# Merged FFN products grouped by their column count, and three small moves at the start of a two-layer decoder trunk

## The chip, the core and the metric

The kernel runs on one core of one Trainium2 chip. The metric is the device time of one execution in microseconds (us). The times given are medians over executions; the profile is of one execution. Engines are named as the profile names them: PE (TensorE) with its weight loads PEld, DVE (VectorE), ACT (ScalarE), POOL (GpSimd) and SP (SyncE). A suffix q, as in SPq, stands for the engine's own queue of issued work, here its DMA issues.

## The reference

The kernel computes two decoder layers on 256 positions of width 1024. Each layer is a half-step SwiGLU FFN, an attention, and a second half-step FFN, each behind an RMS norm whose shift, scale and gate are computed from a vector c:

```python
def swiglu(h, w_gate, w_up, w_down):
    return (jax.nn.silu(h @ w_gate) * (h @ w_up)) @ w_down

c_act = jax.nn.silu(c)
for layer in range(2):
    sh1, sc1, g1, sh2, sc2, g2, sh3, sc3, g3 = jnp.split(c_act @ ada_w[layer] + ada_b[layer], 9, axis=-1)
    h = modulate(rms_norm(x, norm_g[layer, 0]), sh1, sc1)
    x = x + 0.5 * g1 * swiglu(h, ffn_w_gate[layer, 0], ffn_w_up[layer, 0], ffn_w_down[layer, 0])
    h = modulate(rms_norm(x, norm_g[layer, 1]), sh2, sc2)
    x = x + g2 * (moba_attention(h, ...) if layer == 0 else mla_attention(h, ...))
    h = modulate(rms_norm(x, norm_g[layer, 2]), sh3, sc3)
    x = x + 0.5 * g3 * swiglu(h, ffn_w_gate[layer, 1], ffn_w_up[layer, 1], ffn_w_down[layer, 1])
```

The FFN's inner width is 2816. All inputs and weights are float32.

## The kernel before

**Products in parts.** Every float32 matrix that enters a large product is split into a high part hi, rounded to a type that PE takes at full rate, and a rest lo: ACT writes hi (L629), DVE writes lo = raw - hi (L630), both for 128x1024 pieces in `split`. A product is then hi·hi + hi·lo + lo·hi. `mm3` (L759 to L761) issues these as three products.

**Merged blocks.** In the gate and up projections of all four FFNs, once past the first columns, the weights are the stationary operand and the activations h stand beside each other as [h_hi | h_lo], 2 x 256 columns. `mm2` issues one product of 512 columns with the weights' hi part (L863), which gives hi·hi and hi·lo in the two halves of a PSUM tile, and one of 256 columns with the weights' lo part (L864) into the second half. For each of 128 inner columns f there are two sides, gate and up, of KD = 8 contraction steps k each; two values of f share a weight block. Four sides of eight k make a block. `units` then adds the halves (L904, L905), applies Silu (L907), multiplies (L908) and splits again (`split_evac`, L774 and L775).

**Down projection.** The rest of an FFN multiplies the split inner activations by w_down in products of 512 columns, with `mm3`.

**First stage.** `first` computes the first six blocks of 128 inner columns of the first FFN while x and the weights of the shift and scale vectors arrive. It broadcasts Silu(c) over the partitions into c_b with a product (L1531) and two ACT copies (L1532), forms the sums of squares of the two row blocks of x on DVE (L1545), reduces weights against c_b on DVE (L640), and from these makes h (z at L1576) and multiplies it (L1594 to L1596) in products of 256 columns.

**The order of the work.** The program is first written in one order and then ordered anew by a planner, `Order`: it simulates the engines with a table of costs and writes each engine's instructions in the order of that plan. Engines run their queues in that order. Instructions in `held` are not placed before 40 us of the plan (`HELD`); `hold` marks them: the tables of the rotary embedding (`rope_tables`) and `mla_consts`, the products of those tables with gains (L1347) and two masks. `ranked` puts first-stage instructions in a given rank. Loads are issued by SP; a buffer pool `splitp` has eight hi and eight lo tiles, and PSUM has four tiles for these products.

Of the kernel before, what the change touches and what calls it, by code (L numbers as in the profile page):

```python
# [15 lines left out]
AF = mybir.ActivationFunctionType  # L16
ALU = mybir.AluOpType
# [5 lines left out]
D = 1024  # L23
KD = D // P
S = 256
# [15 lines left out]
EPS = 1e-6  # L41
# [145 lines left out]
HELD = 40e3  # L187
# [56 lines left out]
class Order:  # L244
# [120 lines left out]
    def place(self, need):  # L365

        n = len(self.ins)
        left, ready, start, done = list(self.npre), [0.0] * n, [0.0] * n, [0.0] * n
# [26 lines left out]
        def consider(k):  # L395

            r = ready[k]
            for t in self.tiles_of[k]:
                if t not in granted:
                    waiting.setdefault(t, []).append(k)  # L400
                    if t not in asked:
                        asked[t] = True
                        grant(self.ring[t])
                    return
                r = max(r, granted[t] + (WAKE if granted[t] else 0.0))
            if self.ins[k].name in self.held:
                r = max(r, HELD)
            ready[k] = r
            heapq.heappush(known[self.eng[k]], (r, k))

        def choose(e, t):
# [24 lines left out]
        while placed < n:  # L436
            t, e = 1e15, None
            for x in ENGINES:
                if x == "SP" and len(flight) >= FLIGHT:
                    free[x] = max(free[x], flight[-FLIGHT] + 50.0)  # L440
                if avail[x] or known[x]:
                    s = free[x] if avail[x] else max(free[x], known[x][0][0])
                    if s < t:
                        t, e = s, x
            assert e, "no instruction can be placed"
            while known[e] and known[e][0][0] <= t:
                r, k = heapq.heappop(known[e])
# [6 lines left out]
            k = x[1]  # L454
# [18 lines left out]
            for s in self.succ[k]:  # L473
                if self.eng[s] != e or self.dma[k]:
                    r = done[k] + WAKE
                else:
                    r = t + occ if e == "PE" else done[k] + 35.0
# [8 lines left out]
            for u in self.tiles_of[k]:  # L486
                users[u] -= 1
                last_use[u] = max(last_use.get(u, 0.0), done[k])
                r = self.ring[u]
# [34 lines left out]
def trunk(ctx: ExitStack, tc: tile.TileContext, a: dict, out: bass.AP):  # L524
    nc = tc.nc
# [41 lines left out]
    def pe(us):  # L567
        clock[0] += us
        if busy[0]:
            return  # L570
        while pend and pend[0][0] <= clock[0]:
            run_next()
        while pace[0] and clock[0] >= pace[1]:
            pace[1] += pace[0]
            ada(1)
# [4 lines left out]

    first_rank, held, late, last_ffn = {}, set(), set(), []

    @contextmanager
    def noted(names):
        n = len(nc.cur_bb.bb.instructions)
        yield
        names.update(i.name for i in nc.cur_bb.bb.instructions[n:])
# [20 lines left out]
    xs = [cp.tile([P, D], F32, name=f"x{t}") for t in range(NT)]  # L610
# [3 lines left out]
    all_cols = cp.tile([P, 3 * NK + KD + NT + 4 + 2 * RO], F32, name="cols")  # L614
# [5 lines left out]
    cols, cact = all_cols[:, :3 * NK].rearrange("p (i c) -> p i c", i=3), places["c"]  # L620
    m_cols = cp.tile([P, 2, NK], F32, name="m_cols")

    c_b = cp.tile([P, D], F32, name="c_b")
# [24 lines left out]
    ready = set()  # L648
# [208 lines left out]
        both = h[0][3][:, k].rearrange("p i t q -> p (i t q)")  # L857
        return both[:, :S], both[:, S:], both

    def mm2(ps, wh, wl, h, start, stop):  # L860


        nc.tensor.matmul(ps, wh, h[2], start=start, stop=False)  # L863
        nc.tensor.matmul(ps[:, S:], wl, h[0], start=False, stop=stop)  # L864
        pe(0.347)

    def norm_T(t, key, *more):
        h = new_h(t)
        modulate_T(t, [(key, h), *more], rstd_of(t), CHAIN)
# [16 lines left out]
    def ffn(layer, idx, h, after, ada_to, start=None):  # L886

        last = (layer, idx) == (1, 1)
        with ExitStack() as st:
# [4 lines left out]
            def units(f, gate, up=None):  # L894


                g = gp.tile([P, S], F32, tag="gT", name=nm("g"), bufs=2)
                if up is None:
                    gate, up = gate[:, :S], gate[:, S:]
                    nc.scalar.activation(g, gate, AF.Silu)  # L900
                else:
                    u = gp.tile([P, S], F32, tag="uT", name=nm("u"), bufs=1 if start else 2)
                    for x, ps in ((g, gate), (u, up)):
                        nc.scalar.activation(x, ps[:, S:], AF.Copy)  # L904
                        nc.vector.tensor_tensor(x, ps[:, :S], x, op=ALU.add)  # L905
                    up = u
                    nc.scalar.activation(g, g, AF.Silu)  # L907
                nc.vector.tensor_tensor(g, up, g, op=ALU.mult)  # L908
                gh, gl = [gq.tile([P, S], F32R, tag=f"{nme}{f}", name=nm(nme)) for nme in ("gh", "gl")]
                split_evac(gh, gl, g)  # L910
                for t in range(NT):
                    gT[f, t] = kslice(gh, t), kslice(gl, t)
# [6 lines left out]
            for t in range(0 if start else NT):  # L919
                for i, pl in enumerate(parts):  # L920
                    ps = mm_tile()
# [22 lines left out]
            for f0 in range(B1 * P if start else FB, F, S):  # L944
                if f0 == SIDE_TO * S:
                    while start and next(side[0], "end") != "end":
                        bias_step()
                    gq = st.enter_context(tc.tile_pool(name=nm("gp"), bufs=1))
                if start and f0 == ROPE_AT * S:
                    hold(rope_tables)  # L950
                    hold(mla_consts)
                parts = [[], []]
                for f in range(f0 // P, (f0 + S) // P):
                    merged = (layer, idx) in MERGED
                    ps = [mm_tile() for _ in range(1 + merged)]
                    for i, pl in enumerate(parts):
                        for k in range(KD):
                            if len(pl) <= k:
                                pl += nextw()
                            w = [w[:, f * P - f0:(f + 1) * P - f0] for w in pl[k]]  # L960
                            hs = hk_both(h, k)
                            if merged:
                                mm2(ps[i], *w, hs, start=k == 0, stop=k == KD - 1)
                            else:
                                mm3(ps[0][:, i * S:(i + 1) * S], *w, *hs[:2], start=k == 0, stop=k == KD - 1)
                            if start and k in HOOKS and f0 < SIDE_TO * S:
                                bias_step()
                    units(f, *ps)
            for half in range(2):
                acc = [mm_tile() for _ in range(NT)]  # L970
                wl = []
# [223 lines left out]
                yield  # L1195
            drain()

    def hold(fn):

        with noted(held):  # L1200
            fn()

    def bias_step():

        if len(groups) < 2:
            hold(lambda: next(side[0], None))
        if groups:
            later(BIAS_WAIT, groups.pop(0))
# [280 lines left out]
    def first(units):  # L1489
# [5 lines left out]
        with ExitStack() as st:  # L1495
# [15 lines left out]
                    nc.sync.dma_start(w1(k, j), a["first"][k, j])  # L1511

            with ranked(0):
                nc.sync.dma_start(c_b[0:1, :], a["c"])
                nc.sync.dma_start(all_cols, a["cols"])
            for t in range(NT):
                with ranked(t):
                    nc.sync.dma_start(xs[t], a["x"][0, t * P:(t + 1) * P, :])
# [22 lines left out]
            for t in range(NT):  # L1541
                with ranked(1):
                    s = stats[t] = small([P, 1], "ssq0")
                    junk = raws[3 + t]
                    nc.vector.tensor_tensor_reduce(junk, xs[t], xs[t], 1.0 / D, EPS, op0=ALU.mult, op1=ALU.add,  # L1545
                                                   accum_out=s)
                    diag.append(fp.tile([P, P], F32, name=nm("diag")))
                    rs.append(rstd_of(t))
                    nc.scalar.activation(diag[t], ident, AF.Copy, scale=rs[t])
# [20 lines left out]
            for k in range(KD):  # L1570
# [19 lines left out]
                for f in range(B1):  # L1590
                    for i in range(2):
                        c = (2 * f + i) * P
# [55 lines left out]
```

## Time and profile before

| | |
|---|---|
| runs (us) | 1000.14, 1002.26, 1004.02 |
| median (us) | 1002.26 |
| profiled execution (us) | 1002.69 |
| its span in the profile (us) | 1000.9 |
| PE, PEld busy (us) | 986.4, 836.7 |
| DVE, ACT, POOL busy (us) | 850.1, 629.1, 82.5 |
| DMA over the span | 260.53 MB, mean 260 GB/s |

How to read it: a group's row names the line, engine and operation, output and inputs, shapes and count; after the bar come the busy time of the group, the mean of one in ns, and the idle time of the engine before them with what ended it. A timeline row has start and length in us. A row of one line's summary has the count, the shortest, median and longest duration in ns, and the first and last start. A row by windows has the window, its length, the busy time with the count, the granted TensorE clock, the share of the DMA engines and GB/s. Matmuls are pipelined, so their durations overlap.

### The profile page before, as it was taken

How to read it: one execution, taken by the hardware profiler on the slowest of the kernel's cores; microseconds unless marked ns; L12 is line 12 of the kernel's file. 1: busy time of each engine (PE TensorE's matmuls, PEld its weight loads, DVE VectorE, ACT ScalarE, POOL GpSimd, SP SyncE). 2: the span in 40 equal slices, each digit the busy share in tenths (PEclk: the TensorE clock that was granted, in tenths of full speed). 3: DMA queues.
4: the chain of work that ended last, by engine and by line, in shares of the span. 5: the costliest groups of instructions: out<-in, count | busy, mean ns of one | idle time of the engine just before them, and what ended most of it. 6: DMA issues, size and time to landing. Idle time of an engine off the chain costs nothing.

```text
span 1000.9 us, 15247 instructions
## 1 busy us (share of the span) xinstructions
PE 986.4 (99%) x5558; PEld 836.7 (84%) x5558; DVE 850.1 (85%) x1443; ACT 629.1 (63%) x1169; POOL 82.5 (8%) x124
## 2 busy tenths in 40 slices
PE   8999999999999999999999999999999999999998
PEld 6988888878888788888888888888888878888886
DVE  7999999799989899999799999944998789667642
ACT  5688665378755875665367666643879696566521
POOL 3011000022231000000000000000143010000000
PEclk9999999999999999999999999999999999999999
DMA  9978999899786688988988998552343467544630
GB/s 349 405 281 311 332 311 334 303 335 355 267 309 226 239 281 338 335 317 293 367 320 303 343 326 323 210 213 103 105 153 126 170 242 269 204 168 168 229 129 22
DMA packets 54237, 260.53 MB, mean 260 GB/s; under 512 B 6289, under 2 KB 6801, under 8 KB 35986
## 3 DMA queue, kind: packets, MB, share of 16 engines
q1 hardware_dynamic: 52850, 256.06, 70.5%
q0 software_dynamic: 1024, 3.17, 1.1%
q8 instruction: 43, 0.70, 0.3%
q10 hardware_dynamic: 288, 0.33, 0.1%
q14 instruction: 32, 0.26, 0.1%
HBM read 255.34 MB, written 4.19 MB: 259 GB/s over the span
## 4 chain that ended last, share of the span: by engine, by line
PE 78%; issue 9%; DVE 7%; DMA 4%; ACT 1%; POOL 0%; SPq 0%; DVEq 0%; ACTq 0%; POOLq 0%
PE mm L863 23%; PE mm L759 12%; PE mm L761 12%; PE mm L760 12%; PE mm L864 11%; DVE lo L630 2%; PE at L1014 2%; DMA adaw<-in_ada_dram 2%; DMA raw<-in_first_dram 1%; PE at L1070 1%; PE at L1050 1%; PE tr L809 1%; DMA raw<-in_w_dram 1%; PE tr L1169 1%; DVE z L825 0%
## 5 line engine op out<-in xcount | busy, mean ns | idle before, releaser
L630 DVE TENSOR_TENSOR lo<-raw,hi 128x1024 fp32r<-128x1024 f32 (+3 forms) x312 | 369.6, 1203 | 74.9 <-ACT hi L629 71.0
L629 ACT ACTIVATE hi<-raw 128x1024 fp32r<-128x1024 f32 (+3 forms) x312 | 319.2, 1039 | 165.8 <-PE mm L761 126.7
L863 PE MATMUL mm<-h,hi 128*128 128x512 f32 x1120 | 391.8, 397 | 1.1 <-DVE u L905 0.6
L864 PE MATMUL mm<-h,lo 128*128 128x256 f32 x1120 | 306.5, 280 | 0.0
L863 PEld LDWEIGHTS mm<-h,hi 128*128 128x128 f32 x1120 | 208.1, 188 | 48.5 <-DVE u L905 1.1
L864 PEld LDWEIGHTS mm<-h,lo 128*128 128x128 f32 x1120 | 210.1, 188 | 3.5 <-DVE lo L630 0.3
L640 DVE CUSTOM_DVE_ANT_0 adaw<-adaw,c_b,cols 128x1024 f32<-128x1024 f32 x112 | 141.5, 1280 | 2.9 <-DMA adaw<-in_ada_dram 2.8
L759 PE MATMUL mm<-hi,gh 128*128 128x512 f32 x352 | 137.3, 390 | 0.0
L761 PE MATMUL mm<-hi,gl 128*128 128x512 f32 x352 | 137.1, 390 | 0.0
L760 PE MATMUL mm<-lo,gh 128*128 128x512 f32 x352 | 137.0, 389 | 0.0
L759 PE MATMUL mm<-hi,h 128*128 128x512 f32 (+1 forms) x240 | 94.7, 400 | 0.8 <-ACT h L774 0.8
L761 PE MATMUL mm<-hi,h 128*128 128x512 f32 (+1 forms) x240 | 92.6, 391 | 1.6 <-DVE h L775 1.6
L760 PE MATMUL mm<-lo,h 128*128 128x512 f32 (+1 forms) x240 | 93.8, 394 | 0.0
L761 PEld LDWEIGHTS mm<-hi,gl 128*128 128x128 f32 x352 | 66.1, 188 | 13.7
L759 PEld LDWEIGHTS mm<-hi,gh 128*128 128x128 f32 x352 | 66.1, 188 | 13.6
L760 PEld LDWEIGHTS mm<-lo,gh 128*128 128x128 f32 x352 | 66.1, 188 | 13.5
L678 DVE SCALAR_TENSOR_TENSOR acc<-adaw,cols,acc 128x1024 f32<-128x1024 f32 x48 | 61.4, 1279 | 0.5 <-DMA adaw<-in_ada_dram 0.3
L761 PEld LDWEIGHTS mm<-hi,h 128*128 128x128 f32 x240 | 45.1, 188 | 10.6 <-DVE h L775 2.2
L759 PEld LDWEIGHTS mm<-hi,h 128*128 128x128 f32 x240 | 45.0, 188 | 9.5 <-ACT h L774 1.4
L760 PEld LDWEIGHTS mm<-lo,h 128*128 128x128 f32 x240 | 45.1, 188 | 8.0 <-issue 0.2
L904 ACT ACTIVATE g<-mm 128x256 f32<-128x256 f32 x70 | 26.7, 382 | 35.1 <-issue 18.1
L904 ACT ACTIVATE u<-mm 128x256 f32<-128x256 f32 x70 | 26.6, 380 | 35.2 <-PE mm L864 33.9
(230 smaller groups left out, 1242.0 us busy)
## 6 DMA issues: line engine op xcount, KB each, us to landing
raw<-in_w_dram SPq DMA_DIRECT2D x142, 1024.0 KB, 5.5
adaw<-in_ada_dram SPq DMA_DIRECT2D x160, 512.0 KB, 5.7
raw<-in_first_dram SPq DMA_DIRECT2D x24, 256.0 KB, 7.4
raw<-in_w_dram SPq DMA_DIRECT2D x12, 512.0 KB, 3.8
raw<-in_w_dram SPq DMA_DIRECT2D x6, 576.0 KB, 3.8
bias_d<-bt SPq DMA_DIRECT2D x12, 256.0 KB, 5.2
bg<-bias_d POOLq DMA_DIRECT2D x4, 768.0 KB, 6.6
raw<-in_w_dram SPq DMA_DIRECT2D x2, 768.0 KB, 4.2
```

The source lines that it names most:

```text
L629: nc.scalar.activation(hi, src, AF.Copy)
L630: nc.vector.tensor_tensor(lo, src, hi.bitcast(F32), op=ALU.subtract)
L640: nc.vector.tensor_tensor_reduce(wt, wt, c_b, 1.0, cols[:, i, c:c + 1], op0=ALU.mult, op1=ALU.add, accum_out=m_cols[:, i, c:c + 1])
L678: nc.vector.scalar_tensor_tensor(acc, ada_tile(j, k), cact[:, k:k + 1], acc, op0=ALU.mult, op1=ALU.add)
L759: nc.tensor.matmul(ps, lh, rh, start=start, stop=False)
L760: nc.tensor.matmul(ps, lh, rl, start=False, stop=False)
L761: nc.tensor.matmul(ps, ll, rh, start=False, stop=stop)
L809: nc.tensor.transpose(kslice(pt, j), kslice(y, j), ident)
L863: nc.tensor.matmul(ps, wh, h[2], start=start, stop=False)
L864: nc.tensor.matmul(ps[:, S:], wl, h[0], start=False, stop=stop)
L904: nc.scalar.activation(x, ps[:, S:], AF.Copy)
L1014: nc.tensor.matmul(ps3[:, i, :], qTs(e, t), kTs(e, nk), start=bias is not None, stop=bias is not None or i == len(es) - 1)
```

## The change

In merged blocks a side's eight products of 512 columns are issued first and its eight of 256 columns behind them, in place of pairs; `mm2` goes. c and the column vectors are issued by ACT's queue, so that x is the first that SP issues. The sum of squares of the second row block is formed by ACT instead of DVE. `hold` takes a time of its own, and `mla_consts` is held until 130 us of the plan. Since the planner sees a changed program, the order on all engines is worked out anew. Line numbers shift: L863 and L864 become L957 and L965, L1594 to L1596 become L1599 to L1601, L629 and L630 become L627 and L628.

```diff
-            if self.ins[k].name in self.held:
-                r = max(r, HELD)
-            ready[k] = r
+            r = ready[k] = max(r, self.held.get(self.ins[k].name, 0.0))
...
-    def mm2(ps, wh, wl, h, start, stop):
-        nc.tensor.matmul(ps, wh, h[2], start=start, stop=False)
-        nc.tensor.matmul(ps[:, S:], wl, h[0], start=False, stop=stop)
-        pe(0.347)
...
                 if start and f0 == ROPE_AT * S:
                     hold(rope_tables)
-                    hold(mla_consts)
+                    hold(mla_consts, 130e3)
...
                     for i, pl in enumerate(parts):
+                        lows = []
                         for k in range(KD):
...
                             if merged:
-                                mm2(ps[i], *w, hs, start=k == 0, stop=k == KD - 1)
+                                nc.tensor.matmul(ps[i], w[0], hs[2], start=k == 0, stop=False)
+                                pe(0.227)
+                                lows.append((w[1], hs[0]))
...
+                        for k, (w, hk_) in enumerate(lows):
+                            nc.tensor.matmul(ps[i][:, S:], w, hk_, start=False, stop=k == KD - 1)
+                            pe(0.12)
...
-    def hold(fn):
-        with noted(held):
+    def hold(fn, until=None):
+        names = set()
+        with noted(names):
             fn()
+        held.update((n, until or HELD) for n in names)
...
-                nc.sync.dma_start(c_b[0:1, :], a["c"])
-                nc.sync.dma_start(all_cols, a["cols"])
+                nc.scalar.dma_start(c_b[0:1, :], a["c"])
+                nc.scalar.dma_start(all_cols, a["cols"])
...
-                    nc.vector.tensor_tensor_reduce(junk, xs[t], xs[t], 1.0 / D, EPS, op0=ALU.mult, op1=ALU.add,
-                                                   accum_out=s)
+                    if t:
+                        nc.scalar.activation(junk, xs[t], AF.Square, scale=D ** -0.5, accum_out=s)
+                        nc.vector.tensor_scalar(s, s, EPS, None, op0=ALU.add)
+                    else:
+                        nc.vector.tensor_tensor_reduce(junk, xs[t], xs[t], 1.0 / D, EPS, op0=ALU.mult, op1=ALU.add,
+                                                       accum_out=s)
```

2 lines of the change are left out of this document (1 added, 1 removed).

## The prediction

> **What bounds the kernel now.** I read the page first, then the busy time by windows of 20 us, then single stretches of the timeline.
>
> ```profile
> span 1000.9 us, 15247 instructions
> PE 986.4 (99%) x5558; PEld 836.7 (84%) x5558; DVE 850.1 (85%) x1443; ACT 629.1 (63%) x1169; POOL 82.5 (8%) x124
> L863 PE MATMUL mm<-h,hi 128*128 128x512 f32 x1120 | 391.8, 397 | 1.1 <-DVE u L905 0.6
> L864 PE MATMUL mm<-h,lo 128*128 128x256 f32 x1120 | 306.5, 280 | 0.0
> ```
>
> The profiled execution took 1002.69 us; its span is 1000.9, so 1.79 us lie around it. It stands 0.43 us above the median of the runs shown, 1002.26. TensorE (PE) counts as busy in all but 14.5 us of the span, and its two largest groups are the two lines of mm2, 1120 products of 512 columns and 1120 of 256. PE alone can therefore return time: a DVE or ACT operation that goes is worth only what PE waited for it.
>
> ```profile
> 20.00:40.00 20.00, 20.00 (x170) 1.00 1.04 400
> 40.00:60.00 20.00, 19.32 (x134) 1.00 1.02 391
> 120.00:140.00 20.00, 19.40 (x110) 1.00 0.89 301
> ```
>
> From 20 to 40 us PE has no idle time, so whatever moves its first products moves all that follows. Two later stretches of the first FFN do have idle time, 0.68 us in 40 to 60 and 0.60 in 120 to 140.
>
> The means of 397 and 280 ns overlap, since matmuls are pipelined; the price of a product is the distance from one start to the next. The next rows give first the count of L863 with its first and last start in two long stretches, then its count in three windows.
>
> ```profile
> L863 PE MATMUL mm<-h,hi x203: 392/395/395, 369.8 to 439.8; 128*128 128x512 f32 x102
> L863 PE MATMUL mm<-h,hi x194: 395/398/403, 551.8 to 620.0; 128*128 128x512 f32 x194
> 124.00:154.00 30.00, 28.93 (x85) 1.00 0.92 320
> 548.00:620.00 72.00, 72.00 (x205) 1.00 0.91 335
> 836.00:898.00 62.00, 61.69 (x176) 1.00 0.59 215
> ```
>
> A pair (one product of 512, one of 256) costs (439.8 - 369.8)/202 = 0.3465 us in the first stretch and (620.0 - 551.8)/193 = 0.3534 us in the second. Same instructions, same clock (1.00 in all windows), no wait between them: the alternating stream has two paces, 6.9 ns apart. The three windows hold 85 + 205 + 176 = 466 pairs at the slow pace; the other 654 I count as fast, apart from their stalls.
>
> **The change part by part.**
>
> *Order of the products.* Nothing is added or removed: the same 1120 + 1120 products, in runs of eight and eight. What a product costs beside its own kind stands where the kernel already does this: the down projection (512 columns only, three lines in turn) and the first stage (256 columns only).
>
> ```profile
> L759 PE MATMUL mm<-hi,gh x67: 389/389/389, 654.9 to 699.8; 128*128 128x512 f32 x67
> 25.16 0.28 PE L1596 MATMUL mm<-h,wlo 128*128 128x256 f32 x1
> ...
> 28.52 0.28 PE L1596 MATMUL tr<-h,wlo 128*128 128x256 f32 x1
> ```
>
> 512 beside 512: (699.8 - 654.9)/66/3 = 0.2268 us. 256 beside 256: from 25.16 to 28.52 are 28 steps of 0.120. Together 0.3468: the fast pace. Neither of these streams shows a second pace. In the merged stage itself the planner already made some short runs:
>
> ```profile
> 449.91 0.64 PE L864 MATMUL mm<-h,lo 128*128 128x256 f32 x4
> 450.39 0.85 PE L863 MATMUL mm<-h,hi 128*128 128x512 f32 x3
> 451.07 0.28 PE L864 MATMUL mm<-h,lo 128*128 128x256 f32 x1
> 363.07 1.09 PE L863 MATMUL mm<-h,hi 128*128 128x512 f32 x4
> 364.00 0.52 PE L864 MATMUL mm<-h,lo 128*128 128x256 f32 x3
> ```
>
> Four of 256 take 0.48, three of 512 take 0.68: again 0.120 and 0.2267. But four of 512 at 363.07 take 0.93, or 0.2325 each. Bounds: at 0.3468 for all, 466 x 0.0066 = 3.1 us are gained and 654 x 0.0003 = 0.2 lost; at 0.2325 + 0.120 = 0.3525, 466 x 0.0009 = 0.4 are gained and 654 x 0.0060 = 3.9 lost, so +3.5. I take 0.3470, just above the long runs, because a run of eight has one change of length at either end: 466 x 0.0064 - 654 x 0.0005 = 2.7 us gained.
>
> A rule speaks against runs of 256. The Trainium skill, TensorE: Matmul & The Clock Gate, section LDWEIGHTS (loading the stationary operand), prices a weight load at its columns divided by 1.2, 107 ns for 128 columns, about what 256 columns need to stream. In turn, the load for a product of 256 lies under one of 512; in a run it must fit under another 256. The rows at 25.16 to 28.52, each with a weight load of its own, step by 0.120, so here the load fits and the sum stays; were it not hidden, the result is rival D.
>
> *The start.* c and cols leave SP's queue, x goes first; c's and cols' issues move ahead of the table load on ACT; the second row block's sum of squares moves from DVE to ACT.
>
> ```profile
> 0.74 1.28 ACT L1527 ACT_TABLE_LOAD   x1 [0.74 <-PEq L1636]
> 0.74 0.34 SPq L1514 DMA_DIRECT2D c_b<-in_c_dram  x1
> 1.14 0.36 SPq L1515 DMA_DIRECT2D cols<-in_cols_dram  x1
> 1.55 0.89 SPq L1518 DMA_DIRECT2D x<-in_x_dram  x2
> 2.23 1.05 ACT L1527 ACTIVATE c_b<-c_b 1x1024 f32<-1x1024 f32 x1 [0.21 <-DMA c_b<-in_c_dram]
> 3.34 3.78 PE L1531 MATMUL tr<-c_b,ones_r 1*128 1x512 f32 x4 [0.30 <-ACT c_b L1527]
> 5.93 1.23 DVE L1545 CUSTOM_DVE_ANT_0 raw<-x 128x1024 f32<-128x1024 f32 x1 [2.58 <-DMA x<-in_x_dram]
> 7.15 0.60 ACT L1532 ACTIVATE c_b<-tr 128x512 f32<-128x512 f32 x1 [1.11 <-PE tr L1531]
> 8.86 1.28 DVE L640 CUSTOM_DVE_ANT_0 adaw<-adaw,c_b,cols 128x1024 f32<-128x1024 f32 x1 [0.43 <-DMA adaw<-in_ada_dram]
> 13.19 1.22 PE L1594 MATMUL mm<-h,whi 128*128 128x256 f32 x4 [0.71 <-ACT h L774]
> DMA to landing us min/median/max: 4.4/4.8/5.2
> L629 ACT ACTIVATE hi<-raw 128x1024 fp32r<-128x1024 f32 x296 | 308.1, 1057 | 160.6 <-PE mm L761 121.5 <-PE mm L863 26.4 <-DMA raw<-in_w_dram 8.0
> ```
>
> x is issued at 0.74 instead of 1.55, 0.81 us earlier, and all SP's later issues with it; DVE's wait for the weights of c's product at 8.86 could end at 8.05. On the other side ACT now issues for 0.34 + 0.36, so the table load starts near 1.5 and ends near 2.8; Silu of c starts then instead of 2.23, 0.55 later, and PE's broadcast of c (3.34 to 7.12) ends near 7.7. In the instruction order of the changed program ACT's square of x stands ahead of both copies of c_b. The second x was issued near 1.55 + 0.45 = 2.0; issued near 1.2 now, it lands by the longer of the two landings, 5.2, near 6.4; the square costs about the 1.06 us of another ACT operation of 128x1024; the two copies, 0.60 each, follow. c_b is whole near 6.4 + 1.06 + 1.2 = 8.66, and L640, behind it on DVE, starts then instead of at 8.86. L640, its scale, z and h lead to the first product at 13.19. So -0.2 us. The new wait is DVE's: its small addition to the second sum of squares waits for ACT's square, near 7.5, and L640 stands behind it; that is over before c_b is whole. ACT also takes all three splits of the first weights before z instead of two, which I leave to the upper bound. Bounds: the full 0.81 if c_b is not late; +0.6 if the second x lands no earlier than it did (2.0 + 5.2 = 7.2, so c_b at 9.46). Cover of the issues on ACT: it has no other work before c lands; without that they would cost 0.7.
>
> The Trainium skill, DMA: Bandwidth & Descriptors, section Issuing engines are not separate DMA queues, says that a second issuing engine saves only issue time. By it the gain ends at those 0.81; no run here shows two queues in this stage.
>
> *The constants.* mla_consts is held until 130 us in the plan instead of 40.
>
> ```profile
> L1347 DVE TENSOR_TENSOR sink<-rw_sin,cols x4: 168/169/174, 106.7 to 116.6; 128x16 f32<-128x16 f32 x4
> L1347 DVE TENSOR_TENSOR sinq<-rw_sin,cols x4: 177/178/179, 128.7 to 129.0; 128x16 f32<-128x16 f32 x4
>   DVE u L905: 1.7, 3
> ```
>
> Its sixteen small DVE products lay between 106.7 and 129.0 us, about 0.17 us each, and before that the rotary tables; PE and its weight loads waited three times, 1.7 us in all, for DVE's u (L905) to free a PSUM tile. Beyond 130 us DVE takes them beside an unbroken PE. With the 1.28 us square gone from DVE too, at most the idle time of PE in the two windows can return, 0.68 + 0.60 = 1.3. It may also return nothing, since DVE's splits stay. I take 0.4. The planner works the order out anew, but outside the merged products PE's order differs only in the first stage; the attention stages keep theirs, and I put their change at nothing.
>
> Sum: -2.7 - 0.2 - 0.4 = -3.3 us: 999.4 for the profiled execution, 999.0 from the median.
>
> **The rivals.**
>
> *Everything comes through* (A): all pairs as long runs (-3.1, and another 0.3 for the edges of the slow stretches outside the windows, which I put at 45 pairs), x's whole 0.8, PE's whole 1.3: -5.5, 996.8. For it: short runs at 449.91 already have the pace. Against: c_b's path.
>
> *Runs of 512 stay at 0.2325* (B), the other side: the moving operand here is h, not a weight, and the four at 363.07 went at that pace. Place: every side of every merged block; price +3.5 as above; with the other terms +2.9, 1005.2. It decides from a 512-step of 0.230 upwards: 3.3 us over 1120 pairs are 0.0029, on top of the 0.2270 that I take. Against it: three of 512 at 450.39.
>
> *The late low tiles* (C): a lo tile's first half is last read after eight 512s and four 256s of the odd f instead of four pairs: 2.29 instead of 1.39 us into the side, 0.91 later.
>
> ```profile
> ACT hi L629 <- PE mm L863: 28.2, 36, 1.3
> L864 PEld LDWEIGHTS mm<-h,lo 128*128 128x128 f32 x1120 | 210.1, 188 | 3.5 <-DVE lo L630 0.3
> ```
>
> ACT waited 36 times for hi tiles that PE still read, so buffers do run short; hi comes free earlier now, but lo later, and DVE waiting for it holds up the sums u and g behind it, and so PSUM. Eight blocks of the first FFN with two sides each, 0.91 each: at most 14.6 us, 1013.6 with the rest; a quarter of it cancels the forecast's gain. Against: DVE waited for no PE product of L864 before, and lo follows hi by an ACT split of 1.06.
>
> *Runs of 256 bound by the weight load* (D): a load shows 188 ns. If it could not overlap, seven of eight steps would grow from 120 to 188: 980 x 0.068 = 67 us, 1066 with the rest. This is what the LDWEIGHTS rule would lead to if a load could not go on beside the running product. The 0.120 rows speak against it.
>
> **How the numbers follow.** Forecast 0.60, A 0.24, B 0.10, C 0.04, D 0.02. About 0.5%, 5.0 us, is what a measurement of this kernel can tell from no change: its runs lie between 1000.14 and 1004.02. A lies beyond it, and a tenth of the forecast's own chance (runs below their median): faster 0.30. The rest of the forecast and B (0.3% above) are no change by that bound: 0.64. C and D: slower 0.06. The range goes from A less most of the 2.1 us by which the lowest run lies under the median, 995.0, to the unfavourable start (+0.6), no relief of DVE and pairs a third of the way to B, 0.3488 (466 x 0.0046 - 654 x 0.0023 = 0.6 gained): nothing in sum, 1002.3, set at 1002.5. That leaves out B, C and D, 0.16, and a few runs of A.
>
> **What would show it.** Right: L957's and L965's starts step by about 0.227 and 0.120 in every stretch, and no stretch has a pair at 0.3534; the first product of h and whi starts near 13.0; PE's idle time in 40 to 60 and 120 to 140 shrinks. Wrong: 512-steps of 0.2325 (B); DVE's lo waiting for PE's L965 (C); 256-steps over 0.13 (D); or idle time in the attention stages that was not there before.

## The result and the profile after

The changed kernel takes 1000.13 us (median of 22 runs, 999.08 to 1000.78) where the kernel before, run beside it, takes 1001.55 us (22 runs, 999.66 to 1004.02). The ratio is 0.9983, interval 0.9977 to 0.9990: about 1.7 us less by the ratio, 1.4 by the medians. The 1002.26 of the first three runs lay high; the profiled execution of before, 1002.69, is 1.14 us above the longer series' median. The profiled execution of the changed kernel took 1000.38 us with a span of 998.6, 2.3 less than the span before.

From the page of the changed kernel:

```profile
span 998.6 us, 15267 instructions
PE 984.3 (99%) x5558; PEld 837.0 (84%) x5558; DVE 848.7 (85%) x1442; ACT 630.1 (63%) x1171; POOL 82.8 (8%) x124
L957 PE MATMUL mm<-h,hi 128*128 128x512 f32 x1120 | 288.3, 393 | 0.0
L965 PE MATMUL mm<-h,lo 128*128 128x256 f32 x1120 | 162.0, 282 | 0.6 <-DVE lo L628 0.6
```

PE has the same 5558 products and is still busy all but 14.3 us of the span. L965's busy time falls from 306.5 to 162.0 us only because the pipelined records overlap differently; the pace has to be read from the starts, in the timeline of the changed kernel (start, length, line, count):

```profile
570.40 1.11 PE L965 MATMUL mm<-h,lo 128*128 128x256 f32 x8
571.36 2.00 PE L957 MATMUL mm<-h,hi 128*128 128x512 f32 x8
573.20 1.12 PE L965 MATMUL mm<-h,lo 128*128 128x256 f32 x8
574.15 2.00 PE L957 MATMUL mm<-h,hi 128*128 128x512 f32 x8
```

A side takes 574.15 - 571.36 = 2.79 us: eight of 512 take 1.84 (0.230 each) and eight of 256 take 0.95 (0.119 each), 0.3488 us a pair. This is the end of the prediction's range for pairs, not the 0.3470 it took.

The busy time of PE by windows, after:

```profile
20.00:40.00 20.00, 19.96 (x164) 1.00 1.04 399
40.00:60.00 20.00, 18.84 (x129) 1.00 0.95 363
120.00:140.00 20.00, 19.04 (x111) 1.00 0.88 307
```

The two later windows have 1.16 and 0.96 us of idle time, more than the 0.68 and 0.60 before.

The start of the changed kernel, from the timeline (what ended an idle time stands in brackets):

```profile
0.74 0.52 ACTq L1515 DMA_DIRECT2D c_b<-in_c_dram  x1
0.74 0.86 SPq L1519 DMA_DIRECT2D x<-in_x_dram  x2
4.09 3.78 PE L1532 MATMUL tr<-c_b,ones_r 1*128 1x512 f32 x4 [1.05 <-ACT c_b L1528]
7.25 1.25 ACT L1533 ACTIVATE c_b<-tr 128x512 f32<-128x512 f32 x2
8.54 1.28 DVE L638 CUSTOM_DVE_ANT_0 adaw<-adaw,c_b,cols 128x1024 f32<-128x1024 f32 x1 [1.01 <-ACT c_b L1533]
9.74 1.28 DVE L638 CUSTOM_DVE_ANT_0 adaw<-adaw,c_b,cols 128x1024 f32<-128x1024 f32 x1
10.95 0.15 DVE L643 SCALAR_TENSOR_TENSOR m_cols<-m_cols,cols 128x1 f32<-128x1 f32 x1
12.27 1.22 PE L1599 MATMUL mm<-h,whi 128*128 128x256 f32 x4 [0.29 <-ACT h L772]
```

L638 starts at 8.54 behind a late c_b, as forecast (8.66), but the first product comes at 12.27, 0.92 earlier than before instead of 0.2. Only 0.32 of this is L638's earlier start; 0.43 is L643, DVE's short operation behind it, which takes 0.15 us here and 0.58 in the trace of before:

```profile
11.44 0.58 DVE L645 SCALAR_TENSOR_TENSOR m_cols<-m_cols,cols 128x1 f32<-128x1 f32 x1
```

Where the 2.3 us of the two profiled spans lie: 1.6 us were gained by the end of the first FFN, as the starts of its down projection show (first and last of L759 from 140 us on before, of L757 after):

```profile
L759 PE MATMUL mm<-hi,gh x88: 389/389/395, 154.6 to 216.3; 128*128 128x512 f32 x88
```

```profile
L757 PE MATMUL mm<-hi,gh x88: 389/389/397, 153.0 to 214.7; 128*128 128x512 f32 x88
```

Of the three later FFNs, whose merged blocks are 288 pairs each, one lost and two gained. These are the starts of L863 (first and last) and of the first product of L761 behind them, in the second layer's first FFN, for before; then the same for the changed kernel, where the lines are L957 and L759:

```profile
L863 PE MATMUL mm<-h,hi x288: 389/398/476, 543.9 to 646.3; 128*128 128x512 f32 x144
L761 PE MATMUL mm<-hi,gl x88: 389/389/402, 647.1 to 707.2; 128*128 128x512 f32 x88
```

```profile
L957 PE MATMUL mm<-h,hi x288: 387/393/404, 543.0 to 643.8; 128*128 128x512 f32 x144
L759 PE MATMUL mm<-hi,gl x88: 389/389/398, 645.4 to 705.5; 128*128 128x512 f32 x88
```

From the first 512 to the first L761 are 647.1 - 543.9 = 103.2 us before and 645.4 - 543.0 = 102.4 after. Read in the same way, the stages of the three later FFNs are (in us; the experiments' columns are told below):

| stage | before | before, profiled again (before_a) | after | after_pairs | sixteen |
|---|---|---|---|---|---|
| layer 1, second FFN | 102.8 | 102.8 | 103.5 | 102.7 | 103.1 |
| layer 2, first FFN | 103.2 | 101.8 | 102.4 | 103.2 | 102.1 |
| layer 2, second FFN | 103.0 | 101.8 | 102.4 | 103.0 | 102.1 |

In these three the order of the products gave +0.7 - 0.8 - 0.6 = -0.7 us; the forecast was -2.7 over all four FFNs.

### The profile page after: what moved, and what is told of

The parts are those of the page before. It is cut to its first block, busy times and chain, and to the rows that moved or that the text cites. A ratio compares the mean times of both kernels' runs of the same rounds, so it can differ in the third digit from the quotient of the medians.

```text
span 998.6 us, 15267 instructions
## 1 busy us (share of the span) xinstructions
PE 984.3 (99%) x5558; PEld 837.0 (84%) x5558; DVE 848.7 (85%) x1442; ACT 630.1 (63%) x1171; POOL 82.8 (8%) x124
## 4 chain that ended last, share of the span: by engine, by line
PE 79%; issue 9%; DVE 6%; DMA 4%; POOL 1%; ACT 1%; SPq 0%; ACTq 0%; DVEq 0%; POOLq 0%
PE mm L957 23%; PE mm L757 12%; PE mm L759 12%; PE mm L758 12%; PE mm L965 12%; DMA adaw<-in_ada_dram 2%; PE at L1013 2%; DVE lo L628 2%; DMA raw<-in_first_dram 1%; PE at L1069 1%; PE at L1049 1%; PE tr L1168 1%; PE tr L807 1%; DMA raw<-in_w_dram 1%; DVE z L823 0%
## 5 line engine op out<-in xcount | busy, mean ns | idle before, releaser
L628 DVE TENSOR_TENSOR lo<-raw,hi 128x1024 fp32r<-128x1024 f32 (+3 forms) x312 | 368.9, 1199 | 71.8 <-ACT hi L627 63.2
L627 ACT ACTIVATE hi<-raw 128x1024 fp32r<-128x1024 f32 (+3 forms) x312 | 318.7, 1038 | 154.2 <-PE mm L759 124.2
L957 PE MATMUL mm<-h,hi 128*128 128x512 f32 x1120 | 288.3, 393 | 0.0
L957 PEld LDWEIGHTS mm<-h,hi 128*128 128x128 f32 x1120 | 199.9, 189 | 34.8
L965 PEld LDWEIGHTS mm<-h,lo 128*128 128x128 f32 x1120 | 155.3, 190 | 12.8 <-DVE lo L628 0.8
L965 PE MATMUL mm<-h,lo 128*128 128x256 f32 x1120 | 162.0, 282 | 0.6 <-DVE lo L628 0.6
L638 DVE CUSTOM_DVE_ANT_0 adaw<-adaw,c_b,cols 128x1024 f32<-128x1024 f32 x112 | 142.0, 1285 | 2.5 <-DMA adaw<-in_ada_dram 1.5
L757 PE MATMUL mm<-hi,gh 128*128 128x512 f32 x352 | 137.3, 390 | 0.0
L759 PE MATMUL mm<-hi,gl 128*128 128x512 f32 x352 | 137.1, 389 | 0.0
L757 PE MATMUL mm<-hi,h 128*128 128x512 f32 (+1 forms) x240 | 94.7, 400 | 0.8 <-ACT h L772 0.8
L759 PE MATMUL mm<-hi,h 128*128 128x512 f32 (+1 forms) x240 | 92.6, 391 | 1.6 <-DVE h L773 1.6
L759 PEld LDWEIGHTS mm<-hi,gl 128*128 128x128 f32 x352 | 66.1, 188 | 13.8
L757 PEld LDWEIGHTS mm<-hi,gh 128*128 128x128 f32 x352 | 66.1, 188 | 13.3
L759 PEld LDWEIGHTS mm<-hi,h 128*128 128x128 f32 x240 | 45.1, 188 | 10.5 <-DVE h L773 2.1
L757 PEld LDWEIGHTS mm<-hi,h 128*128 128x128 f32 x240 | 45.0, 188 | 9.5 <-ACT h L772 1.4
L772 ACT ACTIVATE gh<-g 128x256 fp32r<-128x256 f32 x76 | 31.4, 413 | 24.4 <-DVE g L899 24.1
```

The costliest lines, as they stand in the source:

```text
L627: nc.scalar.activation(hi, src, AF.Copy)
L628: nc.vector.tensor_tensor(lo, src, hi.bitcast(F32), op=ALU.subtract)
L638: nc.vector.tensor_tensor_reduce(wt, wt, c_b, 1.0, cols[:, i, c:c + 1], op0=ALU.mult, op1=ALU.add, accum_out=m_cols[:, i, c:c + 1])
L757: nc.tensor.matmul(ps, lh, rh, start=start, stop=False)
L759: nc.tensor.matmul(ps, ll, rh, start=False, stop=stop)
L772: nc.scalar.activation(hi, ps, AF.Copy)
```

## The experiments

**Each part alone, and longer runs.** Four kernels on one chip; before there 1001.52 (999.86 to 1003.41, 33 runs).

*group_only*: the grouped order, with the start and the constants as before.

```diff
-                                mm2(ps[i], *w, hs, start=k == 0, stop=k == KD - 1)
+                                nc.tensor.matmul(ps[i], w[0], hs[2], start=k == 0, stop=False)
+                                pe(0.227)
+                                lows.append((w[1], hs[0]))
...
+                        for k, (w, hk_) in enumerate(lows):
+                            nc.tensor.matmul(ps[i][:, S:], w, hk_, start=False, stop=k == KD - 1)
+                            pe(0.12)
```

> The kernel before with the grouped order of the products alone. Theory T (a run of eight 512s and eight 256s has one pace, 0.3488 us a pair, while pairs in turn fall into 0.3465 or 0.3534): 0.3488 in every stretch, the first product of h and whi near 13.2 us as before, 0.7 us faster than the kernel before in the median (1120 pairs, of which some 466 slow ones come down by 0.0046 and 654 fast ones go up by 0.0023), and run times that lie closer together. Rival S (the whole gain of the change is the earlier start): no change within 0.3 us. Rival G (the whole gain is the grouping): 1.7 us faster.

Measured: 1003.57 (1002.81 to 1004.40), ratio 1.0020 [1.0011, 1.0029]: 2.0 us slower, the largest miss of the study. Its PE stops in the first FFN, from its timeline:

```profile
28.32 0.44 PE L1570 MATMUL tr<-ident,y 128*128 128x128 f32 x2 [0.65 <-ACT z L1582]
120.28 2.34 PE L964 MATMUL mm<-h,hi 128*128 128x512 f32 x9 [0.72 <-DVE g L905]
124.02 0.50 PE L689 MATMUL adaps<-lo,ones_r 128*128 128x512 f32 x1 [1.17 <-DVE lo L630]
```

The planner made a new order for this program, and in the first FFN PE now waits 0.65 + 0.72 + 1.17 us. The last down product of that FFN comes at 217.3 instead of 216.3; 0.6 of this 1.0 us is there at the end of the first stage (52.19 for 51.59), whose last loads are issued 0.6 later (see the table under after_c_sp). The rest of the loss was not measured apart. It fits the pace: its three later FFNs take as long as the changed kernel's, 0.6 to 0.7 us longer each than in before_a below. That the medians would come down by 0.7 us was expected, and they went up by 2.0.

*start_only*: c and cols by ACT's queue, x first, the second square on ACT.

```diff
-                nc.sync.dma_start(c_b[0:1, :], a["c"])
-                nc.sync.dma_start(all_cols, a["cols"])
+                nc.scalar.dma_start(c_b[0:1, :], a["c"])
+                nc.scalar.dma_start(all_cols, a["cols"])
...
+                    if t:
+                        nc.scalar.activation(junk, xs[t], AF.Square, scale=D ** -0.5, accum_out=s)
...
```

> The kernel before with c and the column vectors issued by ACT, x first by SP, and the second sum of squares on ACT; pairs in turn as before. Theory T: first product of h and whi near 12.3 us instead of 13.2, and 0.9 us faster in the median, with run times spread as widely as before. Rival S: 1.7 us faster. Rival G: no change within 0.3 us.

Measured: 1001.09 (999.89 to 1002.03), ratio 0.9995 [0.9986, 1.0003]. No change can be told from the times. Its first product comes at 13.46, not at the 12.3 that was expected and later than before. Even so its profile has the last product of the first stage 0.7 us earlier than before (50.86 for 51.59) and the first FFN's last down product 0.5 earlier (215.8).

*hold_only*: the constants held until 130 us.

```diff
-                    hold(mla_consts)
+                    hold(mla_consts, 130e3)
...
```

> The kernel before with mla_consts held until 130 us of the plan, nothing else. Theory T: no change within 0.3 us, since PE's stops in 40 to 60 and at 120 us stay. Rival H (the relief of DVE is worth PE's stops there): 0.6 us or more faster, and PE without a stop near 120 us.

Measured: 1000.57 (999.46 to 1003.11), ratio 0.9993 [0.9985, 1.0002]: inconclusive. The range of its runs, 3.65 us, is as wide as that of the kernel before. In its profile PE's stop near 120 us is gone, but for 0.31 us at 127.21, which is the sign that rival H named; the times are too scattered to say what that is worth.

*sixteen*: as the changed kernel, but the gate's and up's sixteen products of 512 first, then their sixteen of 256.

```diff
+                    lows = []
                     for i, pl in enumerate(parts):
-                        lows = []
...
-                        for k, (w, hk_) in enumerate(lows):
+                    for i, k, w, hk_ in lows:
```

> The changed kernel with both sides' sixteen products of 512 columns first and the sixteen of 256 behind them. Theory T (each change from 256 to 512 costs: the first five 512s behind it take some 28 ns more together, and the first 256 some 8 ns less): half the changes, 70 fewer, 20 ns each, so 1.4 us faster than the changed kernel, near 998.7, with a pair at 0.3477. Rival (the grouped pace is a property of products of h, wherever they stand): no change against the changed kernel. Rival (hi is needed earlier and lo tiles are held longer, so buffers run short): slower than the changed kernel by 1 us or more, with ACT or DVE waiting for the products of 256.

Measured: 999.48 (998.56 to 999.98), ratio 0.9976 [0.9967, 0.9985]. This version is faster than the kernel before by 2.4 us by the ratio, and 0.65 us under the changed kernel by the medians, half of what was expected. The two intervals overlap, so against the changed kernel the times alone do not decide; each of its three later FFNs is 0.3 to 0.4 us shorter in the table above. From its timeline:

```profile
575.90 3.82 PE L955 MATMUL mm<-h,hi 128*128 128x512 f32 x16
579.55 2.08 PE L963 MATMUL mm<-h,lo 128*128 128x256 f32 x16
581.46 3.82 PE L955 MATMUL mm<-h,hi 128*128 128x512 f32 x16
```

Sixteen of 512 take 3.65 us, 0.2281 each, and sixteen of 256 take 1.91, 0.1194 each: 0.3475 a pair. Longer runs have the lower pace.

**One part undone at a time.** Four kernels on another chip; before there 1001.94 (999.46 to 1004.32, 33 runs).

*after_pairs*: the changed kernel with the products in turn again (`mm2`).

> The changed kernel with its pairs in turn again, as before; c on ACT, the square on ACT and mla_consts at 130 us stay. Theory T2 (the grouped order has one pace, 0.3488, about 0.65 us an FFN dearer than pairs that run at 0.3465 and 1.3 cheaper than pairs at 0.3534; the kernel before falls into either, anew in every execution; the gain of the change comes from its start and its held constants): median within 1 us of the changed kernel's 1000.1, lowest run about 1.5 us below the changed kernel's lowest, spread of the runs twice as wide. Rival G (grouping carries the gain): 1 us or more slower than the changed kernel in the median and in the lowest run.

Measured: 1001.48 (999.37 to 1003.30), ratio 0.9997 [0.9988, 1.0006]: 1.4 us of the change's gain go with the order, though the two intervals just overlap. The median was expected within 1 us of the changed kernel's. Its range is 3.9 us wide against 1.7 for the changed kernel, and its lowest run, 999.37, lies no lower than the changed kernel's 999.08, which was not expected: at the fast pace alone it should have been below.

*after_hold40*: constants at 40 us again.

```diff
-                    hold(mla_consts, 130e3)
+                    hold(mla_consts)
```

> The changed kernel with mla_consts held until 40 us of the plan as before. Theory T2 with the relief of DVE as its larger part: 1.5 us slower than the changed kernel, with longer stops of PE between 110 and 130 us, as in the kernel with the grouped order alone. Rival (the constants are worth nothing, the start is all): within 0.3 us of the changed kernel.

Measured: 1000.04 (999.37 to 1000.78), ratio 0.9986 [0.9977, 0.9995]: the held constants are worth nothing that these runs can tell, against an expectation of 1.5 us. Yet its start differs a good deal. From its timeline:

```profile
9.29 0.98 POOL L1354 MEMSET mask<- 128x512 bf16 x2
10.21 1.74 DVE L638 CUSTOM_DVE_ANT_0 adaw<-adaw,c_b,cols 128x1024 f32<-128x1024 f32 x1
10.23 2.19 POOL L1355 TENSOR_SCALAR_AFFINE_SELECT mask<-mask 128x512 bf16<-128x512 bf16 x2
11.88 0.56 DVE L643 SCALAR_TENSOR_TENSOR m_cols<-m_cols,cols 128x1 f32<-128x1 f32 x1
13.60 0.74 PE L1599 MATMUL mm<-h,whi 128*128 128x256 f32 x4 [1.15 <-ACT h L772]
```

With the constants at 40 us POOL builds the two masks just here, and DVE's operations beside it take 1.74 and 0.56 us instead of 1.28 and 0.15 in the changed kernel. The first product comes 1.33 us later (13.60 for 12.27): 0.46 + 0.41 by these two, and 0.46 because the first L638 starts later (9.00 for 8.54). The Trainium skill, SBUF — State Buffer, section Who interferes with whom, says that VectorE and GpSimd share one pair of ports under an exclusive lock. The trace agrees in direction: DVE is longer by 0.46 and 0.41 us beside POOL's L1355, and not beside its MEMSET, where the first L638 took 1.28. That the lock lasts a whole instruction is not shown here, and not every operation is longer: in the kernel before, an L640 from 10.23 on took 1.28 though POOL's operation on the masks ran from 10.80.

*after_dve_sq*: the second square on DVE again.

```diff
-                    if t:
+                    if False:
                         nc.scalar.activation(junk, xs[t], AF.Square, scale=D ** -0.5, accum_out=s)
```

> The changed kernel with the second sum of squares on DVE as before; c on ACT's queue and x first stay. If ACT's square is what delays c_b (prediction's reading), c_b is whole near 7.9 instead of 8.5, L638 starts near 8.1 or when its weights land, and the first product of h and whi comes 0.3 us earlier than 12.27; time within 0.3 us of the changed kernel. Rival (DVE's 1.28 us are what matters): first product later by 0.5 or more and the kernel slower by 0.5 or more.

Measured: 1000.29 (999.36 to 1001.10), ratio 0.9983 [0.9974, 0.9991]: the square's place is worth nothing that these runs can tell. c_b was expected whole near 7.9 and the first product 0.3 earlier; c_b is whole at 8.50 as in the changed kernel, since its second half waits for PE's broadcast of c, and the first product comes at 12.71, 0.44 later. From its timeline:

```profile
7.90 0.60 ACT L1533 ACTIVATE c_b<-tr 128x512 f32<-128x512 f32 x1 [0.23 <-PE tr L1532]
8.53 1.28 DVE L638 CUSTOM_DVE_ANT_0 adaw<-adaw,c_b,cols 128x1024 f32<-128x1024 f32 x1 [0.55 <-ACT c_b L1533]
```

*after_c_sp*: c and cols issued by SP ahead of x again.

```diff
-                nc.scalar.dma_start(c_b[0:1, :], a["c"])
-                nc.scalar.dma_start(all_cols, a["cols"])
+                nc.sync.dma_start(c_b[0:1, :], a["c"])
+                nc.sync.dma_start(all_cols, a["cols"])
```

> The changed kernel with c and the column vectors issued by SP ahead of x, as before; the square on ACT stays. If x's earlier issue is what brings the first product forward (by 0.9 us in the changed kernel): first product of h and whi near 13.0, 0.8 us slower than the changed kernel. Rival (the start does not reach the end, since transfers or DVE bound the first FFN anyway): first product late, but the end within 0.3 us of the changed kernel.

Measured: 1001.94 (1001.23 to 1002.42), ratio 1.0004 [0.9995, 1.0013]: the whole gain is gone, so c's queue is worth 1.8 us by the medians, 2.1 by the ratios, where 0.8 was expected. These are the last six issues of the first weights and, behind them, PE's wait for the first of those weights to be split (whi), from the timelines of before, the changed kernel, after_hold40 and after_c_sp in turn:

```profile
33.80 4.89 SPq L1511 DMA_DIRECT2D raw<-in_first_dram  x6
42.59 0.39 PE L1594 MATMUL mm<-h,whi 128*128 128x256 f32 x1 [0.19 <-ACT whi L1585]
```

```profile
32.87 4.89 SPq L1512 DMA_DIRECT2D raw<-in_first_dram  x6
41.68 0.39 PE L1599 MATMUL mm<-h,whi 128*128 128x256 f32 x1 [0.50 <-ACT whi L1590]
```

```profile
32.81 4.86 SPq L1512 DMA_DIRECT2D raw<-in_first_dram  x6
41.92 0.39 PE L1599 MATMUL mm<-h,whi 128*128 128x256 f32 x1 [0.51 <-ACT whi L1590]
```

```profile
34.03 4.88 SPq L1512 DMA_DIRECT2D raw<-in_first_dram  x6
42.81 0.39 PE L1599 MATMUL mm<-h,whi 128*128 128x256 f32 x1 [0.48 <-ACT whi L1590]
```

| | first product | last six issues | PE goes on behind its wait | last product of the stage |
|---|---|---|---|---|
| before | 13.19 | 33.80 | 42.59 | 51.59 |
| after | 12.27 | 32.87 | 41.68 | 50.72 |
| after_hold40 | 13.60 | 32.81 | 41.92 | 50.91 |
| after_c_sp | 13.74 | 34.03 | 42.81 | 51.85 |
| hold_only | 12.37 | 33.56 | 42.37 | 51.35 |
| group_only | 12.90 | 34.40 | 43.19 | 52.19 |
| start_only | 13.46 | 33.03 | 41.81 | 50.86 |

From PE's wait to the end of the stage all seven take 9.0 us (8.98 to 9.05), and the wait comes 8.8 to 9.1 us behind the issues, whatever the first product did. hold_only and group_only show it best: their first products come 0.82 and 0.29 us earlier than before, and their stages end 0.24 earlier and 0.60 later, as their loads do. In before_a and after_dve_sq PE shows no wait for whi near 42 us, yet their stages too end 17.8 us behind the last six issues (51.67 and 33.88, 50.76 and 32.98). ACT's split waits for the load, and SP's issues wait for landings of earlier loads. In the waits of the changed kernel from 8 to 52 us:

```profile
ACT whi L1590 <- DMA raw<-in_first_dram: 7.8, 7, 2.1
SPq L1512 <- DMA adaw<-in_ada_dram: 12.4, 12, 2.4
```

So near 42 us PE comes down to the pace of the loads: time that PE gained before is given back in this wait, and time that SP's loads gain stays. Both results fit this: a first product 1.33 us earlier is worth 0.19 at the stage's end (after and after_hold40), and loads 1.16 us earlier are worth 1.13 (after and after_c_sp). Why group_only's loads come later than before with the same issues in SP's queue was not traced. Of the 1.9 us by which after_c_sp's first FFN ends later (216.6 for 214.7), the other 0.8 arises behind the stage; near 120 us its timeline has PE stops of 0.40 and 1.13 us where the changed kernel has one of 0.96.

**The kernel before, profiled again, and runs of four.** Another chip; before there 1002.81 (1000.54 to 1003.99, 13 runs).

*before_a* and *before_b* are the kernel before, unchanged, to see whether the slow pairs lie in the same places in each execution.

> The kernel before, unchanged, in another execution. Theory T2: the same program falls into other stretches of slow pairs than in the profile on record (450 of 1120 pairs in groups of six at 0.351 to 0.356 there); its time is near 999.5 plus 0.0069 us for each slow pair. Rival P (the pace belongs to the program: place of its tiles, its waits): the same stretches are slow again, 124 to 154, 548 to 620, 836 to 898.

> The kernel before, unchanged, in a third execution. As for the execution ahead of it: by theory T2 again another count of slow pairs, and a time that follows it; by rival P the same stretches.

Measured: 1000.30 and 1003.00 us, spans 998.5 and 1001.2. L863 in the stretch from 552 to 620 us, in before_a and then in before_b:

```profile
L863 PE MATMUL mm<-h,hi x197: 392/395/395, 552.0 to 619.9; 128*128 128x512 f32 x197
```

```profile
L863 PE MATMUL mm<-h,hi x194: 395/398/403, 551.8 to 620.0; 128*128 128x512 f32 x194
```

A pair takes (619.9 - 552.0)/196 = 0.3464 us in the one and (620.0 - 551.8)/193 = 0.3534 in the other, in the same stretch of the same program. From 840 to 896 both go at 0.3469, where the first profile was slow (160 starts of L863 there, 163 in these two). Counted in groups of six pairs with a pace of 0.351 to 0.356, the three executions of before have 450, 72 and 282 slow pairs of 1120. The expected time, 999.5 + 0.0069 us for each slow pair, gives 1002.6, 1000.0 and 1001.4 where 1002.69, 1000.30 and 1003.00 were measured. The third is 1.6 off. Counted alike, the profiles of start_only (999.89 us), hold_only (999.53) and after_pairs (1001.49), which also have the products in turn, show 12, 18 and 390 slow pairs. Part of before_b's 1.6 us is a stop of PE in the first FFN, here in before_b and then in before:

```profile
124.12 0.50 PE L863 MATMUL mm<-h,hi 128*128 128x512 f32 x1 [1.72 <-DVE u L905]
```

```profile
122.70 0.51 PE L863 MATMUL mm<-h,hi 128*128 128x512 f32 x1 [0.60 <-DVE u L905]
```

It is 1.1 us longer, in the same program. So two things differ from one execution of before to the next; what chooses either was not found.

*fours*: the changed kernel in runs of four and four.

```diff
                                 lows.append((w[1], hs[0]))
+                                if k == KD // 2 - 1:
+                                    for w, hk_ in lows:
+                                        nc.tensor.matmul(ps[i][:, S:], w, hk_, start=False, stop=False)
+                                        pe(0.12)
+                                    lows = []
...
```

> The changed kernel with runs of four in place of eight: a side's first four 512s, their four 256s, then the other four and four. If each change of length costs what the changed kernel shows (512s of 0.234, 0.236, 0.228, 0.233 behind 256s, then a 256 of 0.113): 0.351 us a pair, 2.4 us slower than the changed kernel, near 1002.5. Rival (the pace of a run is set by something other than the changes of length): 0.3488 again and the changed kernel's time.

Measured: 1001.73 (1001.06 to 1004.23), ratio 0.9997 [0.9987, 1.0007]: 1.4 us above the changed kernel by the ratios and 1.6 by the medians, where 2.4 was expected; by the ratios the intervals just overlap. From its timeline:

```profile
575.65 1.09 PE L957 MATMUL mm<-h,hi 128*128 128x512 f32 x4
576.59 0.63 PE L970 MATMUL mm<-h,lo 128*128 128x256 f32 x4
577.06 1.09 PE L957 MATMUL mm<-h,hi 128*128 128x512 f32 x4
...
579.86 1.09 PE L957 MATMUL mm<-h,hi 128*128 128x512 f32 x4
```

Twelve pairs from 575.65 to 579.86: 0.3508 each, with four of 512 in 0.94 or 0.235 each. The rows are rounded to 0.01 us; over all full runs of the traces the medians for four, eight and sixteen are 0.3503, 0.3491 and 0.3479 a pair. They lie 3.5, 2.3 and 1.1 ns above the prediction's 0.3468, which is 14, 18 and 18 ns for each run of 512 with its run of 256: about one price a run. Products in turn change length at every product and yet go at 0.3464 when fast, so this price does not hold for them, and where it comes from is open.

## Why the prediction was right or wrong

The time forecast, 999.0, is 1.1 us under the measured median and the sign is right, but two terms were wrong in size and partly made up for each other. That is luck in part: the sum of the terms, -3.3, is about twice the 1.4 to 1.7 measured, and the 1002.26 from which it was taken lay 0.7 above the median of the longer series.

**Order of the products: mis-sized on both sides.** The step that failed is "the other 654 I count as fast": 466 slow pairs were priced as a property of the kernel. They belong to one execution. before_a, all but free of slow pairs, has its two second-layer stages at 101.8 us; grouped they take 102.4. Against such an execution the grouped order loses 0.6 to 0.7 in each of the three later FFNs, against the first profile it gains 0.8 and 0.6 in two of them. The kernel before draws from both, and its runs spread over 4.4 us for 1.7 of the changed kernel; the executions with many slow pairs are the ones that the change does away with, as the runs' ranges suggest: the lowest of both kernels are 0.6 us apart, the highest 3.2. Undone alone the order costs 1.4 us (after_pairs). The other half of the step, 0.3470 a pair because "a run of eight has one change of length at either end", came out at 0.3488: the first products of 512 behind a product of 256 step by 234, 236, 228, 233 and 231 ns and only from the sixth on by 227, so a run behind a run of 256 costs some 28 ns more, spread over five products, of which the run of 256 behind it returns about 8. The four products at 363.07 (0.2325), which the prediction left to rival B, were the right sample; why the three at 450.39 went at 0.2267 is not known.

**The start: mis-sized, through the path chosen.** c_b was late as worked out (8.54 for 8.66), but in part by luck: PE's broadcast, which ends at 7.87 (4.09 + 3.78), held the second half of c_b as long as ACT's square did, and with the square on DVE c_b came no sooner (after_dve_sq). And c_b's chain did not set the stage. The prediction followed the path to the first product and let that stand for the whole; it held that 20 to 40 us has no idle time of PE, "so whatever moves its first products moves all that follows". But near 42 us PE waits for the first weights, and the stage's end moves with SP's loads of them: these came 0.93 us earlier and the end 0.87. What the prediction took as its far bound, the full 0.81 of SP's issues, is near the 0.87 at the stage's end and below what c's queue alone is worth: 1.13 there and 1.8 to 2.1 at the kernel's end (after_c_sp). The row that speaks of it was in the trace of before, PE's wait of 0.19 us for whi at 42.59; small as it is, it says that PE had caught up with the loads. That the square is on ACT costs nothing that can be told (after_dve_sq).

**The constants: -0.4 forecast; undoing this part alone changed the time by -0.1 us by the medians and +0.3 by the ratios, inside the intervals.** The mechanism that was named, less idle time of PE behind DVE, did not occur in the changed kernel: near 120 us PE stops for DVE's lo there too. With the constants held alone (hold_only) the stop of 0.60 us that before has near 120 us was gone; what that is worth the times do not tell.

```profile
121.42 0.50 PE L687 MATMUL adaps<-lo,ones_r 128*128 128x512 f32 x1 [0.96 <-DVE lo L628]
```

What did occur, no masks on POOL beside DVE at 9 to 13 us, was not foreseen, and most of it was swallowed by the wait for the first weights.

**"Outside the merged products PE's order differs only in the first stage."** For the attention stages, whose change was put at nothing, this held: from the first FFN's last down product to the next merged block are 357.6 - 216.3 = 141.3 us before and 356.0 - 214.7 = 141.3 after. The prediction gave no term to the first FFN behind the first stage, and there it fails. The parts alone give +2.0, -0.5 and -0.7 us by the ratios and together -1.7; undone singly, order, c's queue, constants and square cost 1.4, 2.1, 0.3 and 0. The parts do not add; each program has its own plan and its own stops of PE in the first FFN. Which edit brings which stop was not settled.

**The rivals.** A did not come: runs of eight never reached 0.3468. B came half way: the 512-step averages 0.230, just the point from which it was to decide, but as a cost of the first five products, not as the pace of a run; sixteen gets 0.2281. The time did not go its way. C's wait exists and is small; who waited for L965 in the changed kernel:

```profile
  DVE lo L628: 4.7, 4
```

Four waits, 4.7 us in all; PE itself sat idle before L965 for only 0.6 us. D did not come: the 256-step is 0.119, so the weight load lies under it. Of the marks named, the steps of 512 (0.227 only at a run's end), the first product (12.27 for 13.0) and the idle windows went against the forecast's details; that no stretch shows 0.3534 held.

## What to carry to other kernels

A pace or a stall read from one profiled execution may belong to that execution: compare it with the spread of the runs, and with a second profile, before pricing a change on it. Where an engine is busy nearly throughout a stage, look for the first short wait behind a load: in this kernel's first stage an earlier start was worth little behind it (0.19 of 1.33 us), and an earlier place in the load queue nearly all of itself (1.13 of 1.16). Of the grouped orders the longest runs, sixteen, had the lowest pace, and runs of eight and sixteen the steadier times; products in turn were cheaper still in executions at their fast pace, and dearer in the others.

## What the runs showed of the hardware

- The stream of products of 512 and 256 columns in turn has two paces, 0.3464 and 0.3534 us a pair, and one program takes either in the same stretch from one execution to the next, at a granted clock of 1.00. Runs of eight and sixteen showed only one pace: over all full runs of their traces the median is 0.3491 and 0.3479 us a pair, and nine in ten lie within 0.0003 of it. Where the products are in turn, a kernel's runs spread by 3.5 to 4.9 us (before in its four series, after_pairs, hold_only; start_only with 2.1 is an exception), in runs of eight or sixteen by 1.2 to 1.7 (in runs of four by 3.2, of which one run of ten makes 2.1).
- Behind a run of eight or sixteen products of 256 columns, each of the next five products of 512 costs 1 to 9 ns more than the later ones, about 28 ns in sum.
- Two of DVE's operations took 0.4 to 0.5 us longer while POOL worked on masks of 128x512 (after_hold40): 1.74 us instead of 1.28, and a 128x1 operation 0.56 instead of 0.15. Beside POOL's MEMSET of the same masks the first took 1.28.
